# A two-layer encoder trunk on one TensorE: a fifth raw weight tile, gated rows scaled later, and the first input loaded once

## The chip, the cores and the metric

The kernel runs on one core of a Trainium2 chip. The metric is device time in microseconds of one execution; the median of three runs of the kernel before is 2138.84 us (2135.29 to 2139.83).

## What is computed

The reference is a two-layer encoder on 512 tokens with 2048 channels, all in f32. One layer, cut to what matters (`cat` is the concatenation along the channels):

```python
hn = rms_norm(h, attn_norm)
u, v, z, b, c, hh, zb, q, ckv, kr, zc = split(hn @ w_in)         # 2048 -> 6720 columns
y_a = u * (w_spatial @ rms_norm(v) + b_spatial) * silu(z)         # 512 channels
y_b = b * conv3(c * hh) * silu(zb)                                # 512 channels
y_c = latent_attention(q, rms_norm(ckv) @ w_ukv, kr) * silu(zc)   # 8 heads x 128
y = cat(rms_norm(y_a), rms_norm(y_b), rms_norm(y_c))
h = h + y @ w_out
h = h + sigmoid(rms_norm(h) @ w_gate) * (p @ w_ple)
```

## The kernel before

**Arithmetic.** Every f32 operand is split into a rounded part `hi` and a rest `lo`; a product is three matmuls, hi by hi, hi by lo, lo by hi (`mm3`, L175 to L178). A weight arrives by DMA in a `raw` tile (128x1024, 512 KB), ACT casts it to `whi` (L142), DVE takes the difference `wlo` (L143). There are four `raw` buffers; the load of a fifth waits until DVE has read the first.

**Stages of a layer.** First the blocks c and h of the input projection, over 16 k tiles in 8 turns of two; in layer 0 each turn loads two tiles of x from DRAM (`load0`, L401) and splits them into `xp` or `hi`/`lo`. `X.combine(j)` (L373) makes sums and differences of x tiles j and j + 8 and, in both layers, loads these two tiles again, as `xa` and `xb`, on the POOL queue. Then come six calls of `pair()` (L488), each two 512-column blocks computed with 28 products of 12 matmuls instead of 32; DVE adds raw weights there (L517). The outputs leave through `ev` tiles (tags e1, e5, e7, e2, two buffers each). The sixth pair makes the gate block zc, which goes to DRAM as `zcd`. After it: the kv projection `kv()`, attention over eight heads with matmuls of the output projection put in as fillers (`fillers()`, each reads an `old` tile of the residual and adds it, L1038), the second half of the output projection, and the gate.

**Tasks.** Small work runs beside the pairs, as generators that `step()` advances after each product: `task_conv`, `task_b`, `task_a`, `task_kr`, `task_ck`, `task_y`. `task_b` and `task_a` write gated rows y to `ydram`; `task_y`, beside pair 6, reads them back, multiplies each with a row of token factors `rT` (L839) and splits it into hi and lo (L145, L146), for the fillers. `rT` comes from `tokrow()` (L223): a `diag` tile (tag e1) on DVE, a matmul with ones, a copy by ACT (L230). It is called at the end of `task_b` and of `task_a`.

**Order.** The tile framework schedules the whole program with its own timing model and writes out one fixed order for each engine; each engine runs it in order. DMAs are issued from SP (weights), ACT (x) and POOL (spills, reads back, `old`), and stand in the same orders. A tile of a tag with all buffers in use waits for the last reader of the oldest one, a DMA write included.

Of the kernel before, what the change touches and what calls it, by code (L numbers as in the profile page):

```python
# [11 lines left out]
F32 = mybir.dt.float32  # L12
# [75 lines left out]
def trunk(ctx, tc, xT, pT, pos, freq, pars, rows, wsp, wckv, wv, w512, wq0, wq, wkv, wout, wgate, wple, outT):  # L88
# [41 lines left out]
    sync.dma_start(par, pars)  # L130
# [23 lines left out]
    def wtile(s, tag, dt=F32):  # L154
        return wst.tile([P, W2], dt, tag=tag, name=nm(s), bufs={"R": 4, "raw": 4, "whi": 3, "wlo": 3}[tag])
# [66 lines left out]
    def tokrow(r):  # L222

        d = T("diag", "e1")
        v.tensor_tensor(out=blocks(d), in0=ident.unsqueeze(1).to_broadcast([P, NT, P]),
                        in1=r.unsqueeze(2).to_broadcast([P, NT, P]), op=ALU.mult)
        ps = bank()
        pe.matmul(ps, ones, d, start=True, stop=True)
        rt = lay.tile([P, S], F32, tag="rT", name=nm("rT"), bufs=2)
        a.copy(rt, ps)  # L230
        return rt
# [119 lines left out]
    class Operand:  # L351
# [21 lines left out]
        def combine(self, j, src, L):  # L373

            xa, xb = T("xa", "e1"), T("xb", "e5")
            for x, k in ((xa, j), (xb, j + KD // 2)):
                g.dma_start(x, src[k])
                a.activation(out=x, in_=x, func=AF.Copy, scale=col(L, C_ATTN + k))
            lo, up = slice(0, HS), slice(HS, S)
            v.tensor_tensor(out=xb[:, up], in0=xb[:, up], in1=xa[:, up], op=ALU.subtract)  # L380
            v.tensor_tensor(out=xa[:, up], in0=xa[:, lo], in1=xa[:, up], op=ALU.subtract)
            v.scalar_tensor_tensor(out=xa[:, lo], in0=xb[:, up], scalar=-1.0, in1=xa[:, lo],
                                   op0=ALU.mult, op1=ALU.subtract)
            v.scalar_tensor_tensor(out=xb[:, lo], in0=xa[:, lo], scalar=-1.0, in1=xb[:, lo],
                                   op0=ALU.mult, op1=ALU.subtract)
            self.sa[j], self.sb[j] = splitU(xa), splitU(xb)
# [13 lines left out]

    def load0(k):  # L401
        t = T("x", "e7")
        a.dma_start(t, xT[k])
        X.put(k, t, col(0, C_ATTN + k))
        st.add(t)
# [3 lines left out]
    for L in range(DEPTH):  # L409
# [37 lines left out]
        def first(b):  # L447

            raw = wtile("raw", "raw")
            hi, lo = wtile("whi", "whi", F32R), wtile("wlo", "wlo", F32R)  # L450
            for i in range(2):
                sync.dma_start(kview(raw, i, S, True),
                               w512[L, blk[b], :, 0, :, i * P:(i + 1) * P].rearrange("f p c -> p f c"))
                split(*(kview(x, i, S, True) for x in (raw,)), None, kview(hi, i, S, True), kview(lo, i, S, True))
            return hi, lo

        for kk in range(KD // 2):
            if L == 0:
                load0(2 * kk)
                load0(2 * kk + 1)  # L460
            w = {b: first(b) if L == 0 and kk == 0 else weight(lambda raw: ft(blk[b])[0](kk, raw)) for b in "ch"}
            order = [(b, i) for i in range(2) for b in "ch"]
            for b, i in order if kk + 1 < KD // 2 else sorted(order):
                wh, wl = w[b]
                k = 2 * kk + i
                for t in range(NT):
                    xh, xl = X.plain(k, t)
                    mm3(like(pb[b, t], True), xh, xl, kview(wh, i, S, True), kview(wl, i, S, True),
                        k == 0, k == KD - 1)
            if 2 <= kk:  # L470
                X.combine(kk - 2, src, L)
# [182 lines left out]
        def task_b():  # L654
            st_b = Stat(512)
            got = {}

            def ask(f):
                if f < 4:
                    y = U("yb")  # L660
                    g.dma_start(y, ycd[f])
                    got[f] = get("b", bd, f), y

            ask(0)
            ask(1)
            for _ in range(7):
                yield
            for f in range(4):
                b, y = got.pop(f)
                ps = transpose4(lambda t: b[:, t * P:(t + 1) * P])  # L670
                v.tensor_tensor(out=y, in0=y, in1=ps, op=ALU.mult)
# [4 lines left out]
                ask(f + 2)  # L676
                yield
                yield
                yield
            rows_ab[4] = st_b.row()  # L680


        def task_a():
# [62 lines left out]
            rows_ab[0] = tokrow(rroot(m, NT, 512))  # L746
# [56 lines left out]
        def task_ck():  # L803
            got = []

            def ask(f):
                if f < KR:
                    got.append(T("ck", "e7"))
                    fetch(got[f], ckd, slice(f * P, (f + 1) * P))
# [13 lines left out]
        def task_y():  # L823
# [11 lines left out]
            for i, k in enumerate(order):  # L835
                y = got.pop(i)
                get(i + 2)
                yield
                v.tensor_tensor(out=y, in0=y, in1=rows_ab[k // 4 * 4], op=ALU.mult)  # L839
# [118 lines left out]
        def zside(h, half):  # L958
# [3 lines left out]
            pb = bank("o")  # L962
# [44 lines left out]
        def values(h, half, pt2, z, po):  # L1007
# [9 lines left out]
            v.tensor_tensor(out=y, in0=po, in1=z, op=ALU.mult)  # L1017
            if half:
                ys[8 + h] = splitU(ybuf[0], C(C_OUT + 8 + h))
                st_c.add(ybuf[0])  # L1020
# [9 lines left out]
        def fillers():  # L1030
            for f in range(KD):
                ps = bank("mm")
                w = weight(ftload(wout[L, f], 0))
                for q in range(2):
                    wout_part(f, 0, ps, q, w)
                    if q == 1:
                        t = T("old", "e7")
                        g.dma_start(t, src[f])  # L1038
# [206 lines left out]
```

## Time and profile before

| | |
|---|---|
| median of 3 runs | 2138.84 us (2135.29 to 2139.83) |
| the profiled execution | 2136.51 us; span from first to last instruction 2134.7 us |
| TensorE (PE) busy | 2090.8 us (98%), 9928 matmul records |
| VectorE (DVE) busy | 1477.7 us (69%) |
| ScalarE (ACT) busy | 985.9 us (46%) |
| mean granted TensorE clock | 0.998 of full |
| DMA | 318.42 MB, 149 GB/s over the span |

Where PE is busy 98% of the span, what a change of order can win lies in PE's stops; so the views of use are the waits of PE, its timeline around each stop, and the granted clock after it. A number in square brackets at the end of a row of the timeline is the idle time ahead of it, and behind the arrow what ended it.

### The profile page before, as it was taken

The page shows a single profiled execution, that of the slowest core. Times are in us where ns is not written, and L with a number is a line of the kernel's source. Part 1 is how long each engine was busy: PE and PEld are TensorE (multiplying, and loading weights), DVE is VectorE, ACT ScalarE, POOL GpSimd, SP SyncE. Part 2 cuts the span into 40 slices and gives each one's busy share as a digit, 9 for nine tenths or more (in the row PEclk, how much of TensorE's full clock was granted, in tenths as well). Part 3 has the DMA queues.
Part 4 walks back from the last instruction along what each step waited for, and adds up shares of the span by engine and source line. Part 5 has one row for each costly group of instructions (what it writes and reads, how often), then busy time and mean ns, then how long its engine had stood idle before and what let it go on. Part 6 is the DMA issues. An engine that isn't in the chain of part 4 may idle for free. (4 is left out here: it accounts for less than half of the span.)

```text
span 2134.7 us, 26981 instructions
## 1 busy us (share of the span) xinstructions
PE 2090.8 (98%) x9928; PEld 1764.5 (83%) x9928; DVE 1477.7 (69%) x2116; ACT 985.9 (46%) x1506; POOL 329.2 (15%) x527
## 2 busy tenths in 40 slices
PE   8999999999999999999999999999999999999999
PEld 7877888997888888888888788889878888888887
DVE  6787988778667757654465787788796777575333
ACT  6554456545445434433353544555464544443221
POOL 1111004211322201000011010132112221110000
PEclk9999999999999999999999999999999999999999
DMA  8556446564723425334453465455556234153332
GB/s 276 161 161 207 146 137 196 179 196 150 234 92 120 123 65 173 115 113 133 128 186 124 144 199 157 144 186 181 190 172 209 92 121 129 47 168 114 111 118 70
DMA packets 197541, 318.42 MB, mean 149 GB/s; under 512 B 20080, under 2 KB 119808, under 8 KB 197408
## 3 DMA queue, kind: packets, MB, share of 16 engines
q1 hardware_dynamic: 167568, 222.93, 33.8%
q0 software_dynamic: 27536, 89.56, 12.9%
q10 hardware_dynamic: 2304, 4.20, 0.6%
q8 instruction: 78, 1.28, 0.3%
q14 instruction: 55, 0.45, 0.1%
HBM read 272.33 MB, written 44.30 MB: 148 GB/s over the span
## 5 line engine op out<-in xcount | busy, mean ns | idle before, releaser
L142 ACT CAST whi<-raw 128x1024 fp32r<-128x1024 f32 (+3 forms) x530 | 524.2, 993 | 713.9 <-PE s L178 109.9
L143 DVE TENSOR_TENSOR wlo<-raw,whi 128x1024 fp32r<-128x1024 f32 (+3 forms) x530 | 606.0, 1152 | 237.1 <-ACT whi L142 236.2
L517 DVE TENSOR_TENSOR raw<-raw,raw 128x1024 f32<-128x1024 f32 (+2 forms) x192 | 218.4, 1144 | 88.2 <-DMA raw<-in_w_dram 44.4
L177 PE MATMUL s<-wlo,hi 128*128 128x512 f32 (+2 forms) x656 | 252.0, 384 | 10.0 <-DVE wlo L143 9.7
L178 PE MATMUL s<-whi,lo 128*128 128x512 f32 (+2 forms) x656 | 248.0, 378 | 0.0
L176 PE MATMUL s<-whi,hi 128*128 128x512 f32 (+2 forms) x656 | 231.9, 379 | 4.0 <-ACT whi L142 4.0
L176 PE MATMUL mm<-hi,whi 128*128 128x512 f32 x544 | 213.7, 393 | 2.8 <-ACT hi L145 2.7
L177 PE MATMUL mm<-lo,whi 128*128 128x512 f32 x544 | 213.4, 392 | 0.0
L178 PE MATMUL mm<-hi,wlo 128*128 128x512 f32 x544 | 212.6, 391 | 0.0
L177 PE MATMUL mm<-wlo,hi 128*128 128x512 f32 (+2 forms) x512 | 195.0, 381 | 0.5 <-DVE wlo L143 0.3
L178 PE MATMUL mm<-whi,lo 128*128 128x512 f32 (+2 forms) x512 | 193.8, 378 | 0.0
L176 PE MATMUL mm<-whi,hi 128*128 128x512 f32 (+2 forms) x512 | 180.4, 381 | 2.2 <-DVE old L1039 2.1
L177 PEld LDWEIGHTS s<-wlo,hi 128*128 128x128 f32 x656 | 123.9, 189 | 36.1 <-DVE wlo L143 17.6
L176 PE MATMUL s<-hi,whi 128*128 128x512 f32 x384 | 150.2, 391 | 0.0
L178 PE MATMUL s<-hi,wlo 128*128 128x512 f32 x384 | 149.5, 389 | 0.0
L177 PE MATMUL s<-lo,whi 128*128 128x512 f32 x384 | 149.5, 389 | 0.0
L176 PEld LDWEIGHTS s<-whi,hi 128*128 128x128 f32 x656 | 122.9, 189 | 24.4 <-ACT whi L142 5.8
L178 PEld LDWEIGHTS s<-whi,lo 128*128 128x128 f32 x656 | 124.1, 189 | 18.3 <-issue 0.5
L176 PEld LDWEIGHTS mm<-hi,whi 128*128 128x128 f32 x544 | 102.1, 188 | 24.0 <-ACT hi L145 3.1
L177 PEld LDWEIGHTS mm<-lo,whi 128*128 128x128 f32 x544 | 102.2, 188 | 21.6 <-issue 0.5
L178 PEld LDWEIGHTS mm<-hi,wlo 128*128 128x128 f32 x544 | 102.1, 188 | 21.5 <-issue 0.5
L177 PEld LDWEIGHTS mm<-wlo,hi 128*128 128x128 f32 x512 | 96.1, 188 | 17.4 <-DVE wlo L143 2.9
(314 smaller groups left out, 3855.1 us busy)
## 6 DMA issues: line engine op xcount, KB each, us to landing
raw<-in_w_dram SPq DMA_DIRECT2D x150, 512.0 KB, 4.8
raw<-in_wout_dram SPq DMA_DIRECT2D x64, 512.0 KB, 3.7
raw<-in_wgate_dram SPq DMA_DIRECT2D x64, 512.0 KB, 3.6
raw<-in_wq_dram SPq DMA_DIRECT2D x64, 384.0 KB, 3.7
raw<-in_wckv_dram SPq DMA_DIRECT2D x24, 512.0 KB, 3.7
raw<-in_wv_dram SPq DMA_DIRECT2D x16, 512.0 KB, 3.9
raw<-in_wkv_dram SPq DMA_DIRECT2D x16, 512.0 KB, 4.4
mdram<-old SPq DMA_DIRECT2D x32, 256.0 KB, 2.0
```

The costliest lines, as they stand in the source:

```text
L142: a.copy(hi, src)
L143: v.tensor_tensor(out=lo, in0=src, in1=hi.bitcast(F32), op=ALU.subtract)
L176: pe.matmul(out, lh, rh, start=start, stop=False, **kw)
L177: pe.matmul(out, lh, rl, start=False, stop=False, **kw)
L178: pe.matmul(out, ll, rh, start=False, stop=stop, **kw)
L517: v.tensor_tensor(out=x[:, :n2], in0=x[:, :n2], in1=y[:, :n2], op=ALU.add)
```

## The change

1. A fifth `raw` buffer.
2. Layer 0: `par` is loaded on ACT's queue instead of SP's; the tiles of x stay in their buffers (tags e1, e5) until `X.combine` has used them and aren't loaded a second time; the turns of the first stage go in the order 0, 4, 1, 5, ..., so that both tiles of a combination are there, and after every second turn two combinations are made (in layer 1 this order holds too, with the loads from DRAM kept).
3. The first two weights of layer 0 come as whole tiles (two DMAs of 512 KB instead of four of 256 KB); their splits stay in halves.
4. `task_b` asks for its next `b` tile right after the transposes of the one before; `task_ck` uses tag e2 instead of e7.
5. `task_b` and `task_a` keep only the four token factors (`rB`, `rA`); `tokrow` is called in `task_y`, for the fifth to eighth y again, and `rT` is one of the 60 common tiles.
6. The last head's second half transposes z in a bank of tag s, and splits its output in halves.
7. A filler loads `old` ahead of its matmuls.

```diff
--- before.py
+++ after.py
@@ -127,7 +127,7 @@
     mhalf = cst.tile([P, 32], F32, name="mhalf")
     g.memset(mhalf, -0.5)
     par = cst.tile([P, DEPTH * NCOL], F32, name="par")
-    sync.dma_start(par, pars)
+    a.dma_start(par, pars)
 
     warm = cst.tile([P, 1], F32, name="warm")
     a.activation(out=warm, in_=ones[:, 0:1], func=AF.Square)
@@ -152,7 +152,7 @@
         return hi, lo
 
     def wtile(s, tag, dt=F32):
-        return wst.tile([P, W2], dt, tag=tag, name=nm(s), bufs={"R": 4, "raw": 4, "whi": 3, "wlo": 3}[tag])
+        return wst.tile([P, W2], dt, tag=tag, name=nm(s), bufs={"R": 4, "raw": 5, "whi": 3, "wlo": 3}[tag])
 
     def parts(raw, n, tags=("whi", "wlo")):
 
@@ -226,7 +226,7 @@
                         in1=r.unsqueeze(2).to_broadcast([P, NT, P]), op=ALU.mult)
         ps = bank()
         pe.matmul(ps, ones, d, start=True, stop=True)
-        rt = lay.tile([P, S], F32, tag="rT", name=nm("rT"), bufs=2)
+        rt = U("rT")
         a.copy(rt, ps)
         return rt
 
@@ -372,9 +372,10 @@
 
         def combine(self, j, src, L):
 
-            xa, xb = T("xa", "e1"), T("xb", "e5")
+            xa, xb = (x0.pop(j), x0.pop(j + KD // 2)) if L == 0 else (T("xa", "e1"), T("xb", "e5"))
             for x, k in ((xa, j), (xb, j + KD // 2)):
-                g.dma_start(x, src[k])
+                if L:
+                    g.dma_start(x, src[k])
                 a.activation(out=x, in_=x, func=AF.Copy, scale=col(L, C_ATTN + k))
             lo, up = slice(0, HS), slice(HS, S)
             v.tensor_tensor(out=xb[:, up], in0=xb[:, up], in1=xa[:, up], op=ALU.subtract)
@@ -398,8 +399,10 @@
     st = Stat(D)
     X = Operand()
 
+    x0 = {}
+
     def load0(k):
-        t = T("x", "e7")
+        t = x0[k] = T("x", "e1" if k < KD // 2 else "e5")
         a.dma_start(t, xT[k])
         X.put(k, t, col(0, C_ATTN + k))
         st.add(t)
@@ -447,28 +450,29 @@
         def first(b):
 
             raw = wtile("raw", "raw")
+            ft(blk[b])[0](0, raw)
             hi, lo = wtile("whi", "whi", F32R), wtile("wlo", "wlo", F32R)
             for i in range(2):
-                sync.dma_start(kview(raw, i, S, True),
-                               w512[L, blk[b], :, 0, :, i * P:(i + 1) * P].rearrange("f p c -> p f c"))
                 split(*(kview(x, i, S, True) for x in (raw,)), None, kview(hi, i, S, True), kview(lo, i, S, True))
             return hi, lo
 
-        for kk in range(KD // 2):
+        turns = [kk // 2 + kk % 2 * (KD // 4) for kk in range(KD // 2)]
+        for n, kk in enumerate(turns):
             if L == 0:
                 load0(2 * kk)
                 load0(2 * kk + 1)
-            w = {b: first(b) if L == 0 and kk == 0 else weight(lambda raw: ft(blk[b])[0](kk, raw)) for b in "ch"}
+            w = {b: first(b) if L == 0 and n == 0 else weight(lambda raw: ft(blk[b])[0](kk, raw)) for b in "ch"}
             order = [(b, i) for i in range(2) for b in "ch"]
-            for b, i in order if kk + 1 < KD // 2 else sorted(order):
+            last = n + 1 == len(turns)
+            for b, i in sorted(order) if last else order:
                 wh, wl = w[b]
-                k = 2 * kk + i
                 for t in range(NT):
-                    xh, xl = X.plain(k, t)
+                    xh, xl = X.plain(2 * kk + i, t)
                     mm3(like(pb[b, t], True), xh, xl, kview(wh, i, S, True), kview(wl, i, S, True),
-                        k == 0, k == KD - 1)
-            if 2 <= kk:
-                X.combine(kk - 2, src, L)
+                        n + i == 0, last and i == 1)
+            if n % 2 and not last:
+                X.combine(n - 1, src, L)
+                X.combine(n, src, L)
         cs = []
         for t in range(NT):
             c = U("c")
@@ -653,31 +657,36 @@
 
         def task_b():
             st_b = Stat(512)
-            got = {}
-
-            def ask(f):
+            bs, yv = {}, {}
+
+            def ask(f, d):
                 if f < 4:
-                    y = U("yb")
-                    g.dma_start(y, ycd[f])
-                    got[f] = get("b", bd, f), y
-
-            ask(0)
-            ask(1)
+                    if d is bs:
+                        d[f] = get("b", bd, f)
+                    else:
+                        d[f] = U("yb")
+                        g.dma_start(d[f], ycd[f])
+
+            for f in range(2):
+                ask(f, bs)
+                ask(f, yv)
             for _ in range(7):
                 yield
             for f in range(4):
-                b, y = got.pop(f)
+                b, y = bs.pop(f), yv.pop(f)
                 ps = transpose4(lambda t: b[:, t * P:(t + 1) * P])
+                ask(f + 2, bs)
                 v.tensor_tensor(out=y, in0=y, in1=ps, op=ALU.mult)
                 yield
                 g.dma_start(ydram[4 + f], y)
                 st_b.add(y, ps)
                 yield
-                ask(f + 2)
-                yield
-                yield
-                yield
-            rows_ab[4] = st_b.row()
+                yield
+                ask(f + 2, yv)
+                yield
+                yield
+            rows_ab[4] = lay.tile([P, NT], F32, tag="rB", name=nm("rB"))
+            rpow(st_b.mean(), NT, rows_ab[4])
 
 
         def task_a():
@@ -743,7 +752,9 @@
             m = small(NT, "mean")
             s2 = ss.rearrange("p (t h) -> p t h", h=2)
             v.tensor_tensor(out=m, in0=s2[:, :, 0], in1=s2[:, :, 1], op=ALU.add)
-            rows_ab[0] = tokrow(rroot(m, NT, 512))
+            rows_ab[0] = lay.tile([P, NT], F32, tag="rA", name=nm("rA"))
+            g.tensor_scalar(out=m, in0=m, scalar1=1.0 / 512, scalar2=EPS, op0=ALU.mult, op1=ALU.add)
+            rpow(m, NT, rows_ab[0])
 
         sgu = []
 
@@ -805,7 +816,7 @@
 
             def ask(f):
                 if f < KR:
-                    got.append(T("ck", "e7"))
+                    got.append(T("ck", "e2"))
                     fetch(got[f], ckd, slice(f * P, (f + 1) * P))
 
             ask(0)
@@ -835,8 +846,10 @@
             for i, k in enumerate(order):
                 y = got.pop(i)
                 get(i + 2)
-                yield
-                v.tensor_tensor(out=y, in0=y, in1=rows_ab[k // 4 * 4], op=ALU.mult)
+                if i % 4 == 0:
+                    rt = tokrow(rows_ab[k // 4 * 4])
+                yield
+                v.tensor_tensor(out=y, in0=y, in1=rt, op=ALU.mult)
                 ys[k] = splitU(y, C(C_OUT + k))
                 yield
 
@@ -959,7 +972,7 @@
 
             z = sz[h][:, half * HS:(half + 1) * HS]
             scaled(z, rcs[h][:, 2 * half:2 * half + 2], 2)
-            pb = bank("o")
+            pb = bank("s" if h + 1 == HEADS and half else "o")
             for i in range(2):
                 o = HS + i * P
                 pe.transpose(pb[:, o:o + P], z[:, i * P:(i + 1) * P], ident)
@@ -1015,8 +1028,14 @@
                 _, vhh, vll = kv2[k // 2]
                 mm3(po, vhh[:, c], vll[:, c], ph[:, o], pl[:, o], k == 0, k == NT - 1)
             v.tensor_tensor(out=y, in0=po, in1=z, op=ALU.mult)
+            if h + 1 == HEADS:
+                if half == 0:
+                    ys[8 + h] = U("hi", F32R), U("lo", F32R)
+                o = slice(half * HS, (half + 1) * HS)
+                split(y, C(C_OUT + 8 + h), ys[8 + h][0][:, o], ys[8 + h][1][:, o])
+            elif half:
+                ys[8 + h] = splitU(ybuf[0], C(C_OUT + 8 + h))
             if half:
-                ys[8 + h] = splitU(ybuf[0], C(C_OUT + 8 + h))
                 st_c.add(ybuf[0])
 
         def wout_part(f, half, ps, q, w):
@@ -1031,11 +1050,11 @@
             for f in range(KD):
                 ps = bank("mm")
                 w = weight(ftload(wout[L, f], 0))
+                t = T("old", "e7")
+                g.dma_start(t, src[f])
                 for q in range(2):
                     wout_part(f, 0, ps, q, w)
                     if q == 1:
-                        t = T("old", "e7")
-                        g.dma_start(t, src[f])
                         v.tensor_tensor(out=t, in0=ps, in1=t, op=ALU.add)
                         sync.dma_start(mdram[f], t)
                     yield
```

**The head, on ACT.** ACT's order at the start of the program (`x_104`, `x_114` the first two tiles of x; `raw_125` and `raw_134` or `raw_133` the first weights of blocks c and h). Before:

```order
L145 ACTIVATE xp_106<-x_104,par 128x256
L145 ACTIVATE xp_109<-x_104,par 128x256
L194 ACTIVATE acc_112<-x_104 128x512
L142 CAST whi_126<-raw_125 128x4x128
L403 DMA x_191<-in_xT_dram 128x512
L145 ACTIVATE xp_116<-x_114,par 128x256
L145 ACTIVATE xp_119<-x_114,par 128x256
L197 ACTIVATE sq_122<-x_114 128x512
L142 CAST whi_126<-raw_125 128x4x128
```

Now:

```order
L406 DMA x_104<-in_xT_dram 128x512
L406 DMA x_114<-in_xT_dram 128x512
L142 CAST whi_127<-raw_125 128x4x128 x2
L406 DMA x_189<-in_xT_dram 128x512
L406 DMA x_198<-in_xT_dram 128x512
L142 CAST whi_135<-raw_133 128x4x128 x2
L145 ACTIVATE xp_106<-x_104,par 128x256
L145 ACTIVATE xp_109<-x_104,par 128x256
```

The first split of x stood ahead of all casts; it now stands behind the casts of both first weights.

**The end of pair 6, on POOL.** POOL's order from the loads of the gated rows y to the second load of `old`, layer 0 (`ev_42..` and `ev_45..` are outputs of pair 6, `ms` and `rs` the factors of kv). Before:

```order
L830 DMA y_4589<-ydram 128x512
L830 DMA y_4634<-ydram 128x512
L830 DMA y_4660<-ydram 128x512
L865 DMA zcd_896<-ev_4298 128x512
L865 DMA zcd_896<-ev_4593 128x512
```

Now:

```order
L878 DMA zcd_869<-ev_4232 128x512
L878 DMA zcd_869<-ev_4233 128x512
L878 DMA zcd_869<-ev_4524 128x512
L878 DMA zcd_869<-ev_4525 128x512
L219 TENSOR_SCALAR ms_4790<-ms_4790 128x2
L214 TENSOR_TENSOR rs_4793<-ms_4790,mhalf 128x2
L1054 DMA old_4836<-in_xT_dram 128x512
L1054 DMA old_4920<-in_xT_dram 128x512
L841 DMA y_4499<-ydram 128x512
L219 TENSOR_SCALAR ms_4865<-ms_4865 128x2
L841 DMA y_4522<-ydram 128x512
L841 DMA y_4549<-ydram 128x512
```

Before, all eight loads of y stood ahead of pair 6's first `zcd` write; now five of them stand behind its last and behind two loads of `old`.

**The same place, on PE and DVE.** PE's order now, where the kv matmuls (`s_4876`) end and the fillers (`mm_4829`, `mm_4913`) begin:

```order
L177 MATMUL s_4876<-wlo_4769,hi_4460 128x512
L228 MATMUL tr_4598<-diag_4596,ones 128x512
L178 MATMUL s_4876<-whi_4768,lo_4461 128x512
L176 MATMUL mm_4829<-hi_4622,whi_4832 128x512
L176 MATMUL mm_4913<-hi_4622,whi_4916 128x512
L177 MATMUL mm_4829<-lo_4623,whi_4832 128x512
```

and DVE's order now, up to the rest `lo_4623` of the same y:

```order
L225 TENSOR_TENSOR diag_4596<-ident,rA_3577 128x512
L921 TENSOR_REDUCE ms_4790<-sq_4788 128x2
L852 TENSOR_TENSOR y_4464<-y_4464,rT_4474 128x512
L852 TENSOR_TENSOR y_4466<-y_4466,rT_4474 128x512
L852 TENSOR_TENSOR y_4468<-y_4468,rT_4474 128x512
...
L852 TENSOR_TENSOR y_4499<-y_4499,rT_4474 128x512
L146 SCALAR_TENSOR_TENSOR lo_4591<-y_4499,par,hi_4590 128x512
L852 TENSOR_TENSOR y_4522<-y_4522,rT_4600 128x512
L852 TENSOR_TENSOR y_4549<-y_4549,rT_4600 128x512
L146 SCALAR_TENSOR_TENSOR lo_4623<-y_4522,par,hi_4622 128x512
```

The first filler needs y_4522, the fifth y of DVE's order and the second of the POOL loads behind `old`; before, DVE multiplied and split all eight y between the additions of raw weights in pair 6. In layer 1 the orders read alike.

## Rows read from the trace of the kernel before

**Rows 1.** The page, part 1: busy time of the engine, share, instructions.

```profile
PE 2090.8 (98%) x9928; PEld 1764.5 (83%) x9928; DVE 1477.7 (69%) x2116; ACT 985.9 (46%) x1506; POOL 329.2 (15%) x527
```

**Rows 2.** Waits of PE over the span: us in total, times, longest.

```profile
PE s L177 <- DVE wlo L143: 9.7, 12, 2.1
...
PE tr L345 <- DMA b<-bd: 3.7, 2, 2.6
PE mm L176 <- ACT hi L145: 2.7, 2, 1.3
PE tr L345 <- DMA ck<-ckd: 2.3, 3, 0.9
```

**Rows 3.** Timeline of PE at eight stops: start us, us, instruction, [idle before <-releaser].

```profile
6.62 0.80 PE L176 MATMUL mm<-whi,xp 128*128 128x512 f32 x1 [6.62 <-ACT whi L142]
...
15.27 0.50 PE L176 MATMUL s<-whi,xp 128*128 128x512 f32 x1 [0.57 <-ACT whi L142]
...
145.26 0.50 PE L177 MATMUL s<-wlo,hi 128*128 128x512 f32 x1 [1.04 <-DVE wlo L143]
...
379.34 0.46 PE L177 MATMUL s<-wlo,hi 128*128 128x416 f32 x1 [1.98 <-DVE wlo L143]
...
510.42 0.50 PE L176 MATMUL s<-whi,hi 128*128 128x512 f32 x1 [1.26 <-ACT whi L142]
...
1206.00 0.58 PE L177 MATMUL s<-wlo,hi 128*128 128x512 f32 x1 [2.12 <-DVE wlo L143]
...
1440.45 0.46 PE L177 MATMUL s<-wlo,hi 128*128 128x416 f32 x1 [0.65 <-DVE wlo L143]
...
1505.29 0.45 PE L177 MATMUL s<-wlo,hi 128*128 128x384 f32 x1 [1.23 <-DVE wlo L143]
```

**Rows 4.** Timeline of PE at the end of pair 6, layer 0.

```profile
553.58 0.39 PE L178 MATMUL o<-whi,lo 128*128 128x512 f32 x1
553.80 0.39 PE L176 MATMUL mm<-hi,whi 128*128 128x512 f32 x1
```

**Rows 5.** Windows: stretch, length, busy by engine (PE, PEld, DVE, ACT, POOL), PEclk, DMA, GB/s.

```profile
203.55:207.00 3.45, 3.45 (x17) 2.91 (x18) 2.00 (x3) 1.03 (x2) 1.29 (x2) 1.00 1.00 332
380.26:383.68 3.42, 3.42 (x12) 3.29 (x11) 1.72 (x2) 1.20 (x2) 0.00 (x0) 0.50 0.77 249
1206.29:1209.70 3.41, 3.41 (x9) 2.65 (x9) 1.96 (x3) 0.00 (x0) 0.00 (x0) 0.50 0.65 199
6.62:11.62 5.00, 5.00 (x12) 3.93 (x13) 2.76 (x5) 2.62 (x5) 0.00 (x0) 1.00 1.02 334
```

**Rows 6.** Timeline of DVE ahead of two of the stops.

```profile
142.84 1.23 DVE L517 TENSOR_TENSOR raw<-raw,raw 128x1024 f32<-128x1024 f32 x1 [0.28 <-DMA raw<-in_w_dram]
...
377.32 1.02 DVE L517 TENSOR_TENSOR raw<-raw,raw 128x832 f32<-128x832 f32 x1 [3.13 <-DMA raw<-in_wq_dram]
```

**Rows 7.** Timeline of ACT at the head.

```profile
3.68 0.91 ACT L145 ACTIVATE xp<-x,par 128x256 fp32r<-128x256 f32 x2 [1.01 <-DMA x<-in_xT_dram]
...
14.60 1.14 ACT L142 CAST whi<-raw 128x512 fp32r<-128x512 f32 x2 [3.08 <-DMA raw<-in_w_dram]
```

**Rows 8.** Timeline of POOL after pair 6, layer 0.

```profile
562.10 0.55 POOL L1038 DMA_DIRECT2D old<-in_xT_dram  x1 [2.13 <-DMA zcd<-ev]
...
563.57 0.58 POOL L1038 DMA_DIRECT2D old<-in_xT_dram  x1 [0.29 <-issue]
```

**Rows 9.** The tile y: its operations (ns min/median/max, first and last start), landing of its loads.

```profile
L839 DVE TENSOR_TENSOR y<-y,rT x16: 683/689/691, 500.9 to 1581.0; 128x512 f32<-128x512 f32 x16
L145 ACT ACTIVATE hi<-y,par x16: 717/724/731, 501.7 to 1581.7; 128x512 fp32r<-128x512 f32 x16
L146 DVE SCALAR_TENSOR_TENSOR lo<-y,par,hi x16: 746/750/754, 503.3 to 1586.3; 128x512 fp32r<-128x512 f32 x16
...
DMA to landing us min/median/max: 2.9/3.2/4.7
```

**Rows 10.** The copy of the row of token factors (line 230).

```profile
L230 ACT COPY rT<-tr x8: 573/586/586, 266.7 to 1949.6; 128x512 f32<-128x512 f32 x8
```

## The prediction

> **What bounds the kernel now.** I read the page first. PE is busy for 98% of the span [rows 1], so everything that the change can win is in PE's stops, in the half clock behind some of them, and in the head before the first matmul. Then the waits of PE [rows 2]: the reader is to see that PE waits for splits of weights (DVE's `wlo`), for the reads back of `b` and `ck`, and for the split of an attention output (ACT's `hi`, twice 1.3 us). Then the timeline of PE around the stops [rows 3], which shows six of them in the pairs, and DVE ahead of two [rows 6]: at 377.32 DVE had been idle for 3.13 us until a raw weight landed; at 142.84 for 0.28 us only, so there DVE itself was most of the delay. Last the windows behind the stops [rows 5]: after the stops of 1.98 and 2.12 us the granted clock stands at 0.50 of full, 1.2 GHz, for 3.41 us each; after the longest, of 2.64 us, at 1.00, 2.4 GHz.
>
> **What one stop costs.** A 128x512 matmul lasts 0.39 us in the records and the next starts 0.22 to 0.23 us after its start [rows 4]. After a stop this overlap is missing, so a stop costs its idle time and 0.17 us.
>
> **What goes.**
>
> *The fifth raw tile.* Loads of weights are issued when a raw tile becomes free; with a fifth each is issued one tile earlier. The six stops of the pairs, at 145.26, 379.34, 510.42, 1206.00, 1440.45 and 1505.29, hold 1.04 + 1.98 + 1.26 + 2.12 + 0.65 + 1.23 = 8.3 us [rows 3], with 6 x 0.17 it is 9.3. I take off 0.5 for the one at 145.26, where DVE had hardly waited [rows 6]: 8.8 us. Two of the stops are followed by 3.41 us at half clock [rows 5], which loses half of each: 3.4 us. Together 12.2. Below, the gain could be nothing, if what is late is DVE and not the load; above it is 12.7.
>
> *Reads of b and ck.* `task_b` asks for b(f + 2) right after the transposes of f, instead of behind the write to `ydram` and other steps; `ck` has a tag of its own and its reads no longer wait for an output tile of the pair. Two stops for `b` and three for `ck`: 3.7 + 2.3 us [rows 2], and 5 x 0.17: 6.8 us. What is late next there is nothing that the waits name.
>
> *DVE beside pair 6.* The eight multiplications and splits of y, of 0.69 and 0.75 us each [rows 9], stood between the raw additions of pair 6. The waits of PE for `wlo` are 9.7 us in 12 stops [rows 2]; five of them, 7.0 us, are counted above (the sixth was a wait for `whi`). Of the other seven stops with 2.7 us, five lie in the two pairs 6: 1.9 us and 5 x 0.17, 2.8 us.
>
> *The last head.* Its output is split in halves and its last products come ahead of the fillers: the two waits for ACT's `hi`, 2.7 us [rows 2], and 2 x 0.17, less an estimated 0.5 us in each layer for the lo of the second half, which PE still needs soon: 2.0 us.
>
> Sum of what goes: 12.2 + 6.8 + 2.8 + 2.0 = 23.8 us.
>
> **What comes.**
>
> *The head.* PE starts at 6.62 us now [rows 3]. By the order shown above, ACT makes the first split of x only behind the casts of both whole first weights. The first x had landed at 3.68 us [rows 7]. From there the second x (0.26 MB) and two weights (1.05 MB) have to come, at 334 GB/s as in the stretch that follows [rows 5]: 3.9 us, to 7.6. Then two half casts of the second weight at 0.57 (two took 1.14) and one split at 0.45 us (two took 0.91) [rows 7]: 9.2, an estimate. With the waits between engines I take 9.3. Below: if only the weights count, 8.5. Above: the last of the four half weights was there at 14.60 now [rows 7], behind 1.05 MB of `xa` and `xb`, which are gone (3.1 us at that rate): 11.5, and 1.6 of casts and split, 13.1. I take 9.3, nearest to the rate that the rows show. So 2.7 us later, and the stop of 0.57 + 0.17 at 15.27 [rows 3] goes, since both weights are whole by then: a loss of 2.0 us, between 1.1 and 5.8.
>
> *The first input loaded once* takes 16 loads off POOL's queue. No row of PE's waits names `xa` or `xb` in layer 0, so I cost it at nothing; the space on the DMA engines is in the estimate of the head.
>
> *A new stop after pair 6, in both layers.* This is the term that decides. `tokrow` is now called in `task_y`, its `diag` tile needs a buffer of tag e1, and those are held by outputs of pair 6 until they are written to `zcd`. So the y work moves from beside pair 6 to behind it. The order on POOL shows five of the eight y loads behind two loads of `old`, and these wait for the last `zcd` writes: now, `old` is issued at 562.10, after 2.13 us of waiting for `zcd`, and again at 563.57 [rows 8]. Pair 6 ends at about 553.80 [rows 4]; call that E. PE has 38 matmuls for kv and the token rows: 38 x 0.227 = 8.6 us. The first filler, which needs y_4522, is then ready at E + 8.6. Its load is issued behind the second `old`: E + 9.8, and three issues and a small operation of POOL, 1.3 us: E + 11.1. Landing 3.2 us, the multiplication 0.69, the hi 0.72 [rows 9]: E + 15.7. The lo follows 0.75 us later, of which two matmuls cover 0.45. The stop is 7.1 + 0.3 + 0.17 = 7.6 us.
>
> Below: if `zcd` and y were early, DVE and ACT set it. The first token row is copied at about E + 6.4 (23 matmuls, then the 0.59 us of the copy [rows 10] and its own matmul); DVE then has five multiplications and four rests ahead, 5 x 0.69 + 4 x 0.75 = 6.5, and ACT the hi: E + 13.6, a stop of 5.0. Above: with the slowest landing of 4.7 us [rows 9] it is 9.1.
>
> On the clock: two stops of about 2 us were followed by half clock, one of 2.64 us was not [rows 5]. A stop of 7.6 us is far longer than any of these, so I add one half stretch, 1.7 us. The stop is then worth 9.3 us a layer, 18.6 for both; between 2 x 5.2 = 10.4 (no half clock) and 2 x 10.8 = 21.6.
>
> The Trainium skill, in TensorE: Matmul & The Clock Gate, section "HAM oscillation — how this bites in real kernels", says that a PE that waits long enough between bursts drops to the lower clock and starts the next burst there. By that rule the sum keeps the 1.7 us in each layer, without it the sum is 3.4 us lower; the row after 2.64 us differs from it for a short stop, and no run before has a stop as long as the new one.
>
> *Anything else.* The whole order is made anew. The waits that I have not named stay as they are; for new small ones I add 1.0 us, an estimate between 0 and 3.
>
> **The sum.** -23.8 + 2.0 + 18.6 + 1.0 = -2.2 us. The profiled execution took 2136.5 us (span 2134.7 and 1.8 around it), 2.3 under the median of the runs, 2138.84. On the scale of the median the forecast is 2136.6. About 0.2%, 4.3 us, is what a measurement of this kernel can tell from no change; so the forecast is no measurable change, made of two large terms of opposite sign.
>
> **Rivals.**
>
> *The fifth tile does nothing* (slower). If the raw weights are late because of what SP's queue and the DMA engines do and not for want of a free tile, or if DVE is the late one, the six stops and the half clock stay. For: at 142.84 DVE had waited only 0.28 us for the load [rows 6]. Against: 3.13 us at 377.32. Price: 12.2 us back, -2.2 + 12.2 = +10.0, 2148.8. It decides once less than about half of the 12.2 us comes. This is also the way in which the change would not do what it says.
>
> *The new stop is short* (faster). If `zcd` lands earlier than now, since the weights are further ahead and leave the DMA engines to it, DVE sets the stop: 10.4 us instead of 18.6, 8.2 better: -10.4, 2128.4. For: with a fifth tile the weights are asked for earlier and may be out of the way when `zcd` is written, and the stop of 2.64 us shows that a stop need not cost clock [rows 5]. Against: the two loads of `old` still stand ahead of y on POOL.
>
> *Head and stop at their upper ends* (slower). The first whole weights share the DMA engines with the loads of the next three, and y lands in 4.7 us: 3.8 and 3.0 us more: +4.6, 2143.4. For: the last half weight at 14.60 us [rows 7]. Against: 1.05 MB fewer ahead of it.
>
> **How the numbers follow.** The likeliest case gets 0.40 (its own range, from its bounds of a few us, 2133 to 2140), the fifth tile without effect 0.17, the short stop 0.27, the upper ends 0.16. Faster: 0.10 of the first, 0.25 of the short stop, 0.01 left over, 0.36. Slower: 0.02 of the first, 0.13 of the idle tile, 0.11 of the upper ends, 0.26. Within 0.2%: 0.38. The range for 8 in 10 takes in the short stop and most of the slower cases: 2126 to 2147.
>
> **What would show it.** In the waits of PE of the changed kernel: those for `b` and `ck` gone or under 1 us; no stop over 0.5 us in the second to fifth pair; a stop of 5 to 9 us ahead of the first filler in each layer, ended by `hi` of a y, with half clock behind it; the first matmul between 8.5 and 10 us. I am wrong if that stop is missing or under 3 us, if the stops at the raw weights are still there, or if a new stop over 2 us stands at a place that I have not named.

## The result and the profile after

The changed kernel takes 2152.53 us (median of 4 runs, 2150.61 to 2154.96), the kernel before in the same session 2137.07 us: ratio 1.0072, 95% interval 1.0058 to 1.0087. It is slower by 15.5 us. The forecast, 2136.6 us with a range from 2126 to 2147, was wrong: the time lies above the range, and it moved where no change was forecast.

The profiled execution, page of the changed kernel, the span and part 1:

```profile
span 2148.8 us, 26962 instructions
...
PE 2091.1 (97%) x9928; PEld 1767.2 (82%) x9928; DVE 1483.5 (69%) x2118; ACT 986.9 (46%) x1508; POOL 329.6 (15%) x511
```

PE is as busy as before [rows 1]; the span is 14.1 us longer, so the time lies, net, in PE's idle time. The waits of PE, in the order of rows 2 (us in total, times, longest):

```profile
PE mm L176 <- ACT hi L145: 13.4, 2, 7.1
PE mm L176 <- ACT xp L145: 11.2, 1, 11.2
PE s L177 <- DVE wlo L143: 5.0, 8, 1.1
PE o L176 <- ACT hi L142: 4.4, 2, 2.3
PE tr L345 <- DMA ck<-ckd: 2.8, 2, 2.6
PE mm L177 <- DVE wlo L143: 2.8, 6, 1.1
PE tr L1014 <- ACT e L1001: 2.4, 2, 1.2
```

The first row is the stop after pair 6, once in each layer; it now has the label that the last head's wait had before [rows 2]. The second is the head. The waits for `wlo` fell from 9.7 to 5.0 us, but 2.8 us stand at a second tag of banks (`mm`), which had 0.3 before. The fourth and the seventh are new, at the start of attention. The timeline of PE at six stops, as rows 3:

```profile
11.16 0.79 PE L176 MATMUL mm<-whi,xp 128*128 128x512 f32 x1 [11.16 <-ACT xp L145]
...
466.94 0.45 PE L345 MATMUL tr<-ident,ck 128*128 128x128 f32 x1 [2.61 <-DMA ck<-ckd]
...
567.29 0.79 PE L176 MATMUL mm<-hi,whi 128*128 128x512 f32 x1 [6.36 <-ACT hi L145]
...
605.86 0.33 PE L1014 MATMUL tr<-ident,e 128*128 128x128 f32 x1 [1.21 <-ACT e L1001]
...
610.49 0.39 PE L176 MATMUL o<-hi,kvh 128*128 128x256 f32 x1 [2.16 <-ACT hi L142]
...
1632.16 0.80 PE L176 MATMUL mm<-hi,whi 128*128 128x512 f32 x1 [7.05 <-ACT hi L145]
```

Windows of the changed kernel behind three of them, columns as in rows 5:

```profile
466.94:470.40 3.46, 3.46 (x14) 3.46 (x15) 1.62 (x2) 0.69 (x1) 1.30 (x2) 0.60 1.04 336
...
567.29:572.40 5.11, 5.11 (x13) 3.91 (x14) 4.19 (x7) 3.01 (x6) 0.11 (x1) 0.53 0.40 139
...
1632.16:1637.00 4.84, 4.84 (x11) 3.71 (x12) 3.92 (x6) 2.61 (x6) 0.00 (x0) 0.50 0.32 99
```

Behind each the granted clock is at half (1.2 GHz) for most or all of the window: its mean is 0.60 over 3.46 us, 0.53 over 5.11 and 0.50 over 4.84, which lose 1.4, 2.4 and 2.4 us. With idle time and the 0.17 us of a stop, the two stops after pair 6 cost 6.36 + 0.17 + 2.4 = 8.9 and 7.05 + 0.17 + 2.4 = 9.6 us, 18.5 together. POOL ahead of the first shows the queue that the forecast described (timeline of POOL, changed kernel, as rows 8):

```profile
556.88 0.61 POOL L1054 DMA_DIRECT2D old<-in_xT_dram  x1 [0.69 <-DMA zcd<-ev]
...
558.45 0.54 POOL L1054 DMA_DIRECT2D old<-in_xT_dram  x1 [0.96 <-DMA zcd<-ev]
558.98 0.54 POOL L841 DMA_DIRECT2D y<-ydram  x1
560.03 0.62 POOL L219 TENSOR_SCALAR ms<-ms 128x2 f32<-128x2 f32 x1 [0.52 <-DVE ms L921]
560.71 0.58 POOL L841 DMA_DIRECT2D y<-ydram  x1
```

Both loads of `old` wait for `zcd`, and the y that PE needs first is asked for at 560.71. It lands 5.0 us later, and DVE waits for it (timeline of DVE):

```profile
565.79 1.43 DVE L852 TENSOR_TENSOR y<-y,rT 128x512 f32<-128x512 f32 x2 [0.21 <-DMA y<-ydram]
```
The stops at the start of attention have two causes, both in ACT's timeline:

```profile
603.33 0.38 ACT L919 ACTIVATE sq<-mm 128x256 f32<-128x256 f32 x1 [3.92 <-PE mm L178]
603.74 1.28 ACT L1001 ACT_TABLE_LOAD   x1
605.03 0.69 ACT L1001 ACTIVATE e<-s,mx 128x512 f32<-128x512 f32 x1
...
609.34 0.63 ACT L941 ACTIVATE sq<-qn 128x512 f32<-128x512 f32 x1 [0.59 <-DMA qn<-qd]
609.87 0.57 ACT L142 CAST hi<-tr 128x512 fp32r<-128x512 f32 x1
```

The exponentials wait for a table load of 1.28 us with no matmuls left between scores and transposes to cover it; the load itself stands behind a square of kv outputs, for which ACT had waited 3.92 us. The cast that PE needs at 610.49 stands behind a square of `qn`, whose DMA had landed only then: POOL issued that load 605.98 us into the span, against 586.93 in the kernel before (timelines of POOL, changed kernel, then before). It stands there behind the factors made from that same square of kv outputs.

```profile
605.98 0.82 POOL L443 DMA_DIRECT2D qn<-qd  x1
```

```profile
586.93 0.81 POOL L440 DMA_DIRECT2D qn<-qd  x1
```

None of these lines of code is in the change. The order differs. PE's order in the changed kernel, layer 0, ahead of the first transposes (`mm` is kv, `s` the scores, `tr` the transposes of the exponentials):

```
L177 MATMUL mm_5239<-wlo_5135,hi_4460 128x512
L178 MATMUL mm_5239<-whi_5134,lo_4461 128x512
L995 MATMUL s_5019<-krh_3741,q_4994 128x512
L996 MATMUL s_5019<-krl_3742,q_4994 128x512
...
L1014 MATMUL tr_5079<-ident,e_5027 128x128
```

In the kernel before (and in e1 below) the twelve kv matmuls stand behind the score matmuls and so cover the table load, which ACT starts ahead of the square of their output. ACT and PE in the kernel before, the first kv matmul and the first transposes:

```profile
593.73 1.28 ACT L988 ACT_TABLE_LOAD   x1
```

```profile
594.05 0.39 PE L176 MATMUL mm<-whi,hi 128*128 128x512 f32 x1
...
596.77 0.38 PE L1001 MATMUL tr<-ident,e 128*128 128x128 f32 x2
```

### The profile page after: what moved, and what is told of

Its sections match the earlier page's. It is cut to its first block, busy times and chain, and to the rows that moved or that the text cites. A ratio compares the mean times of both kernels' runs of the same rounds, so it can differ in the third digit from the quotient of the medians.

```text
span 2148.8 us, 26962 instructions
## 1 busy us (share of the span) xinstructions
PE 2091.1 (97%) x9928; PEld 1767.2 (82%) x9928; DVE 1483.5 (69%) x2118; ACT 986.9 (46%) x1508; POOL 329.6 (15%) x511
## 3 DMA queue, kind: packets, MB, share of 16 engines
q0 software_dynamic: 26256, 85.37, 12.3%
q8 instruction: 78, 1.28, 0.3%
## 4 chain that ended last, share of the span: by engine, by line
PE 75%; issue 11%; DVE 6%; DMA 5%; POOL 2%; ACT 1%; DVEq 0%; POOLq 0%; SPq 0%; ACTq 0%
PE mm L177 10%; PE mm L176 10%; PE mm L178 10%; PE s L177 9%; PE s L178 9%; PE s L176 9%; PE o L177 3%; PE o L176 3%; PE o L178 3%; DMA raw<-in_w_dram 2%; DVE wlo L143 2%; PE tr L345 1%; DVE raw L521 1%; PE tr L176 1%; PE tr L177 1%
```

## The experiments

Differences are between medians, each first taken against the kernel before run in the same session (its medians were 2135.63 to 2137.5 us).

**e1: the diag tile out of tag e1.** The changed kernel, one edit:

```diff
-        d = T("diag", "e1")
+        d = U("diag")
```

> The changed kernel, with the diag tile of the token rows taken from the 60 common tiles instead of tag e1; nothing else. Theory A (the y work went behind pair 6 only because diag waits for pair 6's outputs, and the stops of 1.2 and 2.2 us at the start of attention come from the order that this late y work led to): both stops after pair 6 go (2 x 9.6 us with their half clock), the stops in attention go (some 6 us for both layers), DVE's stops beside pair 6 come back (3 us): about 2130 us. Rival B (the y work costs PE the same wherever it stands, since DVE is short of time beside pair 6 too): 2145 us or more.

Measured: 2130.39 us, ratio 0.9965 (0.9954 to 0.9976): 6.6 us faster than before, 22.0 faster than the changed kernel. All eight loads of y stand ahead of `zcd` again and both stops are gone, and with them those at the start of attention. Waits of PE in e1:

```profile
PE s L177 <- DVE wlo L143: 7.7, 11, 1.9
...
PE tr L345 <- DMA b<-bd: 2.2, 1, 2.2
...
PE tr L345 <- DMA ck<-ckd: 1.6, 2, 1.4
```

The waits for `wlo` in this row are 2.7 us longer than in the changed kernel, but those at bank tag mm are 1.4 us shorter (1.4 against 2.8), so the y work beside pair 6 costs 1.3 us there, not A's 3. Theory A holds otherwise, and B falls.

**e2: four raw tiles in the changed kernel.**

```diff
-bufs={"R": 4, "raw": 5, "whi": 3, "wlo": 3}[tag])
+bufs={"R": 4, "raw": 4, "whi": 3, "wlo": 3}[tag])
```

> The changed kernel with four raw tiles; the y work still waits for diag. Theory A: the stops after pair 6 stay (2 x 9.6 us), the order at the start of attention goes back (6 us better), the fifth tile is lost (some 5 us worse, half of what was forecast for it): 2149 to 2153 us. Rival C (the fifth tile is worth the 12 us forecast): 2157 us or more. Rival D (it is worth nothing): 2146 us.

Measured: 2160.26 us, ratio 1.0110 (1.0094 to 1.0126), 7.8 us slower than the changed kernel, although the stops at the start of attention are gone (some 6 us better). My theory was wrong here on the fifth tile: net it is worth 7.8 us in this place, and an estimated 14 with those 6 added, more than rival C's 12.

**e3: e1 with four raw tiles** (both edits above).

> As e1_diag_own, with four raw tiles: the fifth tile alone, beside e1. Theory A: 5 us slower than e1, the six stops at raw weights of the kernel before are back, at least four of them. Rival C: 12 us slower than e1. Rival D: the same time as e1 within 2 us.

Measured: 2149.52 us, ratio 1.0059 (1.0042 to 1.0076): 19.1 us slower than e1. Theory A's 5 us is out, C's 12 too. The waits of PE for weights are 24.5 us in e3 (18.0 + 4.0 for `wlo`, 2.5 for `whi`) against 9.1 in e1, and those for `ck` 6.2 against 1.6.

**e4: e1 with the first weights in halves** (`first()` as before, two DMAs for each weight).

> As e1_diag_own, with the first two weights of layer 0 loaded in halves again (four DMAs of 256 KB), the input still loaded once. Theory A (the first matmul waits for both whole weights): it starts at 7 to 8.5 us instead of 11.2, and the time is 2 to 3.5 us under e1. Rival E (the head is late because par, x and the weights share the DMA engines, whatever the pieces): first matmul at 10 us or later, and the time of e1 within 1 us.

Measured: 2128.76 us, ratio 0.9961 (0.9947 to 0.9976); the first matmul starts at 8.46 instead of 11.1 us, as A said. Against its own runs of before it is 8.2 faster, e1 is 6.6: 1.6 us, under the 2 to 3.5 expected and no more than the runs of one kernel differ by, so a gain in time is not shown. At 8.46 it is still 1.8 us later than before [rows 3], so the pieces of the weight aren't the whole cause. E's condition, 10 us or later, fails.

**e5: late token rows alone.** The kernel before, with `tokrow` called in `task_y` as in the change, diag in e1, four raw tiles.

```diff
-            rows_ab[4] = st_b.row()
+            rows_ab[4] = lay.tile([P, NT], F32, tag="rB", name=nm("rB"))
+            rpow(st_b.mean(), NT, rows_ab[4])
...
+                if i % 4 == 0:
+                    rt = tokrow(rows_ab[k // 4 * 4])
```

> The kernel before with one part of the change alone: the token rows made in task_y, with diag in tag e1; four raw tiles. Theory A: the y work goes behind pair 6 by itself, a stop of 5 to 7 us with half clock behind it in each layer (2 x 9.6 us), DVE's stops beside pair 6 go (3 us), and nothing changes at the start of attention: 2137 + 16 = 2153 us. Rival B (the stop needs the rest of the change, the early load of old or the fifth tile): under 2146 us.

Measured: 2149.62 us, ratio 1.0068 (1.0052 to 1.0083), 14.0 us slower, where A had 16. The stop in both layers, timeline of PE in e5:

```profile
567.65 0.80 PE L176 MATMUL mm<-hi,whi 128*128 128x512 f32 x1 [5.96 <-ACT hi L145]
...
1632.55 0.80 PE L176 MATMUL mm<-hi,whi 128*128 128x512 f32 x1 [5.36 <-ACT hi L145]
```

This part alone makes the stop; neither `old` loaded early nor the fifth tile is needed (B falls). The waits for `wlo` did not get shorter with the y work gone from pair 6, as A had it: they are 10.8 + 2.8 us in e5 against 9.7 + 0.3 before. At the start of attention nothing is new here, and nothing in e2: those stops appeared only where late y work and five raw tiles stood together (the changed kernel and, in layer 1 alone, e9 below).

**e6 and e7: the fifth tile alone, on the stages of before.** e6 is e5 with `d = U("diag")`; e7 is e6 with `"raw": 5`.

> As e5, with the diag tile among the 60 common tiles: the y work stands beside pair 6 again, four raw tiles. It is the base for e7. Theory A: the time of the kernel before within 3 us (2134 to 2140 us). Rival B: over 2145 us.

> As e6, with a fifth raw tile: the fifth tile alone, on the stages of the kernel before. Theory A': it is worth the 19 us that e1 and e3 show also here: 2118 us. Rival C (12 us as forecast, since in e3 the other parts of the change made the raw weights later than in the kernel before): 2125 us. Rival D: within 3 us of e6.

Measured: e6 2141.44 us, ratio 1.0025 (1.0013 to 1.0037), 5.8 us slower than before, a little outside A's range: the y work beside pair 6 now makes waits for weights (PE's stops over 0.3 us at weights in the two pairs 6 hold 8.6 us, 2.8 before). e7 2121.45 us, ratio 0.9930 (0.9913 to 0.9946): the fifth tile is worth 20.0 us, near the 19 of A', and C falls. The two profiled executions differ by 16.3 us. Waits of PE in e6:

```profile
PE s L177 <- DVE wlo L143: 14.6, 15, 2.6
...
PE s L176 <- ACT whi L142: 4.7, 5, 1.7
PE mm L177 <- DVE wlo L143: 3.8, 6, 0.9
PE tr L345 <- DMA b<-bd: 2.5, 2, 1.4
```

and in e7:

```profile
PE s L177 <- DVE wlo L143: 8.6, 10, 1.4
...
PE mm L177 <- DVE wlo L143: 2.0, 3, 1.1
...
PE s L176 <- ACT whi L142: 1.7, 1, 1.7
```

23.1 us of waits for weights became 12.3; the waits for `b` and, 1.7 us of them, for `ck` are not in e7's list at all, though `ck` lies in an output tag in that run too (tag e7, as in the kernel before). A fifth tile helps reads that have nothing to do with weights. How it does that (other order on POOL, or other times) was not taken apart.

**e8 and e9: ck among the common tiles.** One edit, on e4 (e8) and on the changed kernel (e9):

```diff
-                    got.append(T("ck", "e2"))
+                    got.append(U("ck"))
```

> As e4_diag_own_halves, with the ck tiles among the common tiles instead of tag e2. Theory A (ck in tag e2 waits for the qd writes of the pair before it, and its reads collide with them): the waits for ck, 3.8 us in e4, go, 3.5 to 5 us better than e4: 2124 to 2125 us. Rival F (the reads of ck are late because of the DMA engines, whatever tile they have): the stops stay, 2128 us.

> The changed kernel with the ck tiles among the common tiles, nothing else: late y work, five raw tiles. Theory A (tag e2 costs what e4 and e8 show): the waits of PE for ck (2.8 us) and the half clock after the one of 2.6 us go, 3 to 7 us better than the changed kernel, 2146 to 2150 us. Rival F (the reads of ck cost nothing here, because the stop after pair 6 waits longer anyway): 2152 us.

Measured: e8 2118.73 us, ratio 0.9925 (0.9908 to 0.9943), 8.7 us better than e4, each against its own runs of before. e9 2141.80 us, ratio 1.0023 (1.0011 to 1.0035), 11.2 us better than the changed kernel. Both are more than expected; F falls. With the waits for `ck` (3.8 us in e4, 2.8 in the changed kernel) those for `b` go too (1.9 and 1.8): neither e8 nor e9 has one. Why `b` gains was not taken apart. Landing of the tile ck's loads in the changed kernel, and in e8:

```profile
DMA to landing us min/median/max: 4.0/6.3/7.1
```

```profile
DMA to landing us min/median/max: 3.3/4.8/5.7
```

Tag e2 is that of outputs of the pair, so ck waited for their `qd` writes, and its reads then took 6.3 us against 4.8. The kernel before had that wait as well, in tag e7: in both, POOL stood idle for 3.7 us in two waits for `qd` writes ahead of loads of ck; in e8 it has none. In e9 not all is ck: against the changed kernel's profile (spans 2148.8 and 2140.0 us) the waits for ck and the half clock behind are 4.2 us, the wait for `b` is 1.8, the stop after pair 6 is 1.6 shorter (11.8 us for both), and the order at the start of attention went back in layer 0 and stayed in layer 1, 3.3 us; the waits for weights are 1.1 us longer.

**e10: e1 with par on SP's queue.**

```diff
-    a.dma_start(par, pars)
+    sync.dma_start(par, pars)
```

> As e1_diag_own, with par loaded on SP's queue again; the first weights stay whole. Theory A (par ahead on ACT's queue delays both loads of x behind the load of ACT's table, and with it the first split): the first split of x stands ahead of the casts again; the first matmul at 7 to 9 us, 2 to 4 us better than e1: 2127 us. Rival G (the whole weights alone make the head late): first matmul at 10 to 11 us, the time of e1.

Measured: 2126.91 us, ratio 0.9956 (0.9941 to 0.9970), 4.0 us better than e1, each against its own runs of before; the two intervals overlap, so the size is rough. Timeline of PE and, below, of ACT in e10:

```profile
6.73 0.79 PE L176 MATMUL mm<-whi,xp 128*128 128x512 f32 x1 [6.73 <-ACT whi L142]
```

```profile
0.74 0.41 ACTq L406 DMA_DIRECT2D x<-in_xT_dram  x1
...
3.71 0.51 ACT L145 ACTIVATE xp<-x,par 128x256 fp32r<-128x256 f32 x1 [1.04 <-DMA x<-in_xT_dram]
```

With whole weights and par off ACT's queue PE starts where it did before. The late head came with the place of `par`, and whole weights alone don't make it: G falls, and so does my own reading of the head. Halves move the first matmul too, to 8.46 us in e4, but only while `par` stands on ACT's queue; with `par` on SP's, whole weights start at 6.73 and halves at 7.84 (e12 below).

**e11 and e12: the good parts together.** e11 is e7 with ck among the common tiles and the last head of the change. e12 is e8 with par on SP.

> The kernel before with the fifth raw tile, the late token rows with their own diag tile, ck among the common tiles and the last head in halves: the parts of the change that were shown or look good, without the input loaded once, the new order of the first stage, the whole first weights and the new order of task_b. Theory A (these parts add up): e7 less the two stops of the last head (2 x 1.8 us): 2118 us. Rival H (what the last head gains is lost in new stops): 2121 us or more.

> The changed kernel with its own diag tile, the first weights in halves, ck among the common tiles and par on SP's queue: e8 with the head of the kernel before. Theory A: the first matmul at 6 to 7 us instead of 9.1, 2 to 3 us better than e8: 2116 us. Rival G (the head is late because the x loads share the DMA engines with the weights): the time of e8 within 1 us.

Measured: e11 2116.78 us, ratio 0.9907 (0.9893 to 0.9922); e12 2117.88 us, ratio 0.9912 (0.9897 to 0.9927), 2.7 us better than e8 by the medians, with overlapping intervals, and the first matmul at 7.8 us, later than the 6 to 7 expected. H falls; the 2.7 us speak against G. Both beat both kernels, by some 20 us against the one before; between them there is no difference that these runs can tell. So the input loaded once, the new order of the first stage, the new order of `task_b` and `old` loaded early, which only e12 has, together bring nothing measurable here; apart they were not run. The two longest waits of PE in e11, whose list has no row for `b` or `ck`:

```profile
PE mm L176 <- ACT whi L142: 6.7, 1, 6.7
PE s L177 <- DVE wlo L143: 6.5, 10, 1.9
```

## Why the prediction was wrong

The runs give a ledger, each step against the runs of before in its own session: the token rows in `task_y` with a diag tile of their own +5.8 (e6), the fifth raw tile -20.0 (e7), all other parts of the change +7.6 (e1 against e7), and the diag tile in tag e1 +22.0 (the changed kernel against e1). Each step starts where the one before it ends, so the sum has to be the measured +15.5, but for rounding; what a step is worth depends on where it is taken. On the stages of before the diag tile in tag e1 costs 8.2 (e5 against e6), and in the changed kernel the fifth tile is worth 7.8 (e2). Of the +7.6, par costs about 4 (e10) and the tag of ck 8.7 (e8); without these two the other parts gain about 5, and e12, with both mended and the first weights in halves, is 5.4 better than e7.

By the forecast's own steps:

- **The new stop after pair 6: right in mechanism; that the size fits is in part luck.** Forecast 7.6 us and 1.7 for the clock, 18.6 for both layers; the profile has 18.5. It is a little shorter (6.4 and 7.0), and the half clock behind it is longer, a loss of 2.4 us each. In layer 0 two misses nearly cancel: kv starts at an estimated 552.3 (the stop's start, 560.93, less the forecast's 8.6), so the load of y_4522, issued at 560.71, comes 8.4 us behind it and not 11.1, since the last `zcd` write landed earlier; and it takes 5.0 us to land, more than the forecast's slowest case of 4.7. e5 shows that the late rows alone make the stop, e1 that the tag is its cause. The rule of the Trainium skill that was weighed there ("TensorE: Matmul & The Clock Gate", "HAM oscillation — how this bites in real kernels") is a drop to the lower clock after a long wait; the trace agrees, with 0.53 and 0.50 of full behind the two.
- **"Anything else", 1.0 us: the first step that failed.** The start of attention waits 1.21 + 2.16 and, in layer 1, as much again: 4.4 + 2.4 us in the waits, less 0.46 us in each layer of before, 5.9 us. The forecast took every wait that it did not name as unchanged. It rested on the orders at the head and at the end of pair 6; this is another place, in code that the diff does not touch. It is also the new stop over 2 us at an unnamed place that the prediction gave as a sign of being wrong.
- **Reads of b and ck, -6.8: failed.** I wrote that ck had a tag of its own; e2 is a tag of the pair's outputs, as e7 was. The waits are 2.8 us for ck (2.3 before) and 1.8 for b (3.7 before), and 1.4 of half clock came: in place of 6.0 us of waits, 6.0. e8 puts a price of 8.7 on the tag, the wait for `b` included.
- **The head, +2.0: under-sized, and its cause was wrong.** PE starts at 11.16 us, not 9.3: a loss of 4.5 less the 0.7 of the stop that went, 3.8. ACT's order with the first split behind both casts, on which the step rested, came with `par` on ACT's queue: in e10 PE starts at 6.73.
- **The fifth raw tile, -12.2: right in sign, mis-sized; DVE beside pair 6, -2.8: too large.** In the changed kernel the waits for weights fell from 9.7 + 4.6 and some 0.3 to 5.0 + 2.8 + 0.2 us, and the two half-clock stretches of 1.7 each are gone: about 10 us against 15 for both terms. New stops stand at `wlo` for bank tag mm, where there was 0.3 us. The part of DVE is 1.3 us by e1 against the changed kernel, and e5 shows no gain at all. On the stages of before the tile is worth 20.0 us, more than I gave it, for it also ends waits for b and ck; in the change these came back, and e8 and e9 show that they go with the tag of ck.
- **The last head, -2.0: right** within what can be seen; its two waits for `hi` are gone.

Attention 5.9, b and ck 6.8, the head 1.8, the weights 5, less the 1.0 that I had allowed for: some 18.5 us, against 16.3 between the forecast and the change of the profiled span (14.1 + 2.2); sums of waits come no closer than that. Of the rivals, "the fifth tile does nothing" is refuted by e3 and e7, "the new stop is short" by the profile; "head and stop at their upper ends" had the head partly right. None of them was the case: the two failures that cost most, attention and ck, stood in no rival.

What stays open: why the scheduler moves the kv matmuls ahead of the last score matmuls when late y work and a fifth tile come together, and not always then (in layer 0 of e9 it does not). That the order did it is shown by profile and order; the reason is not.

## What to carry to other kernels

A tile's tag is a queue: who takes a tag that pair outputs hold waits for their DMA writes, so in this bundle a diag tile of 256 KB cost 22 us and a ck tile 9, and one word of code gave each back. The price hangs on the rest: on the stages of before the diag tile cost 8, and in run e7 ck in an output tag made PE wait nowhere. Where a scheduler writes the order, compare the order over the whole span and not only at the edited lines, above all what now stands between a table load or a late DMA and the instruction that PE waits for. And test parts of a bundle apart: here one part gained 20 us and three together lost more, and the bundle with those parts mended is 20 us faster than the start.

## What the runs showed that I had not expected

How long a stop lasts does not tell by itself whether half clock follows. In the kernel before, stops of 1.98 and 2.12 us were followed by it and one of 2.64 us was not [rows 5]; in e1 one of 1.94 us ahead of 212.41 was, and one of 2.16 us ahead of 1251.86 was not (windows of e1 behind the two, columns as in rows 5):

```profile
1251.86:1256.00 4.14, 4.14 (x22) 3.52 (x23) 2.12 (x4) 1.44 (x4) 0.75 (x1) 1.00 0.81 257
212.41:217.00 4.59, 4.59 (x13) 3.63 (x14) 4.56 (x8) 0.40 (x1) 0.55 (x1) 0.63 0.58 189
```

A small DMA in front of ACT's queue (par, 74 KB) moved the first split of x from 3.71 us (e10) to 10.53 (e1), by way of the order that was built around it.
